# Issuing the mixer's pieces by an account of every tile's writes, reads and transfers

## The chip, the cores and the metric

The kernel runs on one core of a Trainium2 chip. It is one launch, and the time is the device time of that launch in microseconds (us). The core's engines run their own instruction streams in order and meet through semaphores: PE (the tensor engine, matmuls), DVE (the vector engine), ACT (the scalar engine), POOL (GpSimd) and SP, which here only issues DMA transfers. What is compared is the median of several runs of the kernel before and of the changed one.

## The reference

One block of an encoder on 16 meta tokens and 1024 frames of width 1024, in float32. The change lies in the token mixer, of which this is the core:

```python
def token_mixer(u, w_in, ..., w_out):
    proj = u @ w_in                       # q, k, v, o, gates of 4 mLSTM heads; q, k, v, g of 4 retention heads
    qk = silu(causal_dwconv(concat([ml_q, ml_k]), ml_conv_w))
    h_ml = mlstm_chunkwise(q, k, v, li, lf)            # li, lf: log gates, from 4 + 4 columns of proj
    h_ml = sigmoid(ml_o) * head_norm(h_ml, ml_norm_g)
    rq, rk = rotary(rt_q, pos), rotary(rt_k, pos)
    h_rt = retention_chunkwise(rq, rk, rv, log_gamma)
    h_rt = silu(rt_g) * head_norm(h_rt, rt_norm_g)
    return concat([h_ml, h_rt]) @ w_out
```

A gated feed-forward part (width 2816, with a causal convolution) and a last norm follow. They are not touched.

## The kernel before

**Products.** Every matrix product is done in float32 out of reduced-precision pieces: a matrix is split into a high part (an ACT cast, L365) and a low part (DVE, the matrix less its high part, L370), and a product takes three matmuls, high x high, low x high and high x low (L772, L773, L774). The large products use a seven-product scheme (Winograd's form of Strassen's): seven weights `hi_*`/`lo_*`, made from four quarters by sums (L443, L444, L447, L448 for one head's weights), meet seven right factors `uS1` to `uS4` and others. One **step** is one of those products over one range of tokens: 12 matmuls into one PSUM bank. `evac` (L838 to L844) then takes the bank away: a copy on ACT (L840, L842) for products 0, 6, 2, 3, a sum or difference on DVE (L844) for the rest.

**Stages.** After the input norm (to about 80 us) comes the mixer, head after head in the order 4, 0, 1, 2, 3, 5, 6, 7, where 0 to 3 are mLSTM heads and 4 to 7 retention heads. PE's steps run in a fixed order: `o` (the output gate of a head, banks `po4x`, `po4y`, ...), `q` (q and k of the next, `pq0x`, ...), `vp` (v of two heads, `pv1x`, ...), and so on; then the out-projection (`pwx`), up and gate, and down-projection, to the end.

**Pieces.** Between the steps goes all the rest, as **pieces**: the weight splits (`quartered`, L429ff, seven parts per weight); the convolution and Silu that make `qT` and `kT` (`qk_tasks`, L1001 to L1043); a retention head's rotary tables or an mLSTM head's decay tables (tiles `A`, loaded by `tables_load` L958, used by `tables_tasks`); the gate chain `gates()` (L1060ff, which on PE shows as the small tiles `pg`, `pe`, `pf` and `pt`); the chunkwise scan, `scan_a` (scores `s`, weighted scores `pt`) and `scan_b`; the head norm and, behind it, the transposes `tr` with the copies `mx` out of their one PSUM bank; sums of rows of `w_out` (`raw_w`, L515 to L519, stored back to DRAM as `wsw`); and two small groups on PE (`pvm` L596 and `pm`) that read a transferred weight unsplit.

**The order.** The program is written out by Python that runs once, and the order in which it emits the instructions is the order in which each engine runs them; no engine overtakes. `go` (L1567ff) takes the next PE step, and `slot` around it decides which pieces come ahead of and behind it. `tick` moves the weight pieces in `pend` and the pieces in `front` by one stage each; `side` holds the scan's pieces in a list, each with a condition. All of it goes by an **account**: `watch` sees every instruction and adds a time for it to a running sum for PE, DVE or ACT (`load`), so that `load["DVE"] - load["PE"]` tells how far DVE would be behind. It knows nothing of which tile an instruction reads. What is ready is stated by constants: a key in `done` holds from `max(load DVE, load ACT) + 0.3` on, a transfer is taken as landed after 4 us of PE work (`landed(4, ...)`) and a table after 9, the transpose bank as free 0.9 after the DVE sum, and the weights' own pieces wait only until their transfer was issued (`jwait`). Where a step needs a weight that isn't split yet, `need` (L385) sets `rush` and runs all the pieces there are, until that weight is there. `jload` issues the weight transfers on SP as soon as one of four buffers is free.

## Time and profile before

| | |
|---|---|
| runs, us | 1585.54, 1585.11, 1582.67; median 1585.11 |
| profiled execution, us | 1583.99, its span 1581.8, granted clock 0.98 of full |
| busy of the span | PE 95%, weight load 86%, DVE 69%, ACT 48%, POOL 5% |
| chain of work that ended last | PE 83%, DVE 7%, DMA 6%, ACT 3%, issue 1% |
| moved by DMA | 223.80 MB, mean 141 GB/s over the span |

In rows of the profile, `out<-in` are the tiles that an instruction writes and reads, with the numbers left out that tell apart the buffers of one name; L is the line in the program; `[4.09 <-DMA A<-rot_d]` behind a row is the idle time of its engine just before it, and what ended it. A row of the timeline begins with its start and its duration in us. SPq is SP's queue, in which rows are DMA issues, not transfers.

### The profile page before, as it was taken

Reading aid. Unit: us, or ns where it says so; the run is one execution under the profiler, and the core shown is the slowest. Engines: PE = TensorE matmul, PEld = TensorE weight load, DVE = VectorE, ACT = ScalarE, POOL = GpSimd, SP = SyncE. Lnnn points to the kernel's source line nnn. Section 1 sums busy time; section 2 is a strip of 40 time slices with the busy share of each in tenths; the row PEclk is TensorE's granted clock in tenths of the full one; section 3 lists DMA queues with packets and bytes.
Section 4 is the critical chain, followed back from the end, with each engine's and each line's share of the span. In section 5 each row is a group of like instructions: output and inputs, shape, how many; then the busy total and the mean of one; then the engine's idle time right before and its main releaser. Section 6 shows DMA issues by size and latency. Waiting matters only on the chain.

```text
span 1581.8 us, 25443 instructions
## 1 busy us (share of the span) xinstructions
PE 1505.7 (95%) x9929; PEld 1363.8 (86%) x9929; DVE 1093.4 (69%) x2107; ACT 756.6 (48%) x1454; POOL 72.3 (5%) x133
## 2 busy tenths in 40 slices
PE   7968998899899998998999999999999999999997
PEld 6958998899889998887787989999999999888887
DVE  7765686667775766583776878777666666678657
ACT  5445544545455454555344556444444444334443
POOL 1000000000000000000000000222220000000000
PEclk9979999999999999999999999999999999999998
DMA  6012245234632344469532416888883223943313
GB/s 224 1 59 77 77 138 187 81 97 126 200 112 78 110 150 153 133 231 374 187 120 77 147 51 207 211 219 205 196 190 99 80 81 97 386 142 100 95 52 107
DMA packets 104585, 223.80 MB, mean 141 GB/s; under 512 B 10520, under 2 KB 33760, under 8 KB 104288
## 3 DMA queue, kind: packets, MB, share of 16 engines
q1 hardware_dynamic: 95872, 199.02, 37.4%
q0 software_dynamic: 8448, 23.07, 7.3%
q8 instruction: 78, 1.28, 0.3%
q14 instruction: 43, 0.35, 0.1%
q10 hardware_dynamic: 144, 0.07, 0.0%
HBM read 178.05 MB, written 67.15 MB: 155 GB/s over the span
## 4 chain that ended last, share of the span: by engine, by line
PE 83%; DVE 7%; DMA 6%; ACT 3%; issue 1%; SPq 0%; DVEq 0%; ACTq 0%
PE pdx L774 3%; PE pdx L773 3%; PE pdx L772 3%; PE pup_x L773 2%; PE pup_x L774 2%; PE pup_x L772 2%; PE pga_x L772 2%; PE pga_x L773 2%; PE pga_x L774 2%; PE pdy L774 2%; PE pdy L773 2%; PE pdy L772 2%; PE pwx L774 2%; PE pv L812 2%; PE pwx L772 2%; PE pwx L773 2%
## 5 line engine op out<-in xcount | busy, mean ns | idle before, releaser
L656 ACT CAST hi_up<-raw_up 128x512 fp32r<-128x512 f32 (+1 forms) x52 | 36.5, 719 | 107.0 <-PE pga_z L773 60.2
L772 PE MATMUL pup_x<-uh_g,hi_up 128*128 128x256 f32 (+1 forms) x240 | 67.8, 285 | 1.2 <-ACT uh_g L1758 1.2
L773 PE MATMUL pup_x<-ul_g,hi_up 128*128 128x256 f32 (+1 forms) x240 | 67.9, 284 | 0.1
L657 DVE TENSOR_TENSOR lo_up<-raw_up,hi_up 128x512 fp32r<-128x512 f32 (+1 forms) x52 | 41.2, 808 | 38.4 <-ACT hi_up L656 37.7
L657 DVE TENSOR_TENSOR lo_ga<-fraw_ga,hi_ga 128x512 fp32r<-128x512 f32 (+1 forms) x52 | 41.8, 807 | 37.1 <-ACT hi_ga L656 36.9
L774 PE MATMUL pup_x<-uh_g,lo_up 128*128 128x256 f32 (+1 forms) x240 | 66.7, 284 | 0.0
L657 DVE TENSOR_TENSOR lo_d<-rd,hi_d 128x1024 fp32r<-128x1024 f32 (+1 forms) x34 | 37.6, 1112 | 32.8 <-ACT hi_d L656 32.7
L656 ACT CAST hi_ga<-fraw_ga 128x512 fp32r<-128x512 f32 (+1 forms) x52 | 36.4, 719 | 45.5 <-PE pup_z L773 24.1
L774 PE MATMUL pdx<-uh_d,lo_d 128*128 128x512 f32 (+1 forms) x156 | 57.9, 375 | 0.0
L773 PE MATMUL pdx<-ul_d,hi_d 128*128 128x512 f32 (+1 forms) x156 | 57.8, 374 | 0.0
L656 ACT CAST hi_d<-rd 128x1024 fp32r<-128x1024 f32 (+1 forms) x34 | 32.3, 959 | 49.4 <-PE pdy L773 32.5
L774 PE MATMUL pdy<-uh_d,lo_d 128*128 128x512 f32 x132 | 51.9, 393 | 0.0
L773 PE MATMUL pdy<-ul_d,hi_d 128*128 128x512 f32 x132 | 51.8, 392 | 0.0
L772 PE MATMUL pdx<-uh_d,hi_d 128*128 128x512 f32 (+1 forms) x156 | 48.5, 372 | 0.0
L772 PE MATMUL pdy<-uh_d,hi_d 128*128 128x512 f32 x132 | 47.9, 389 | 0.0
L772 PEld LDWEIGHTS pup_x<-uh_g,hi_up 128*128 128x128 f32 x240 | 45.9, 191 | 2.3 <-ACT uh_g L1758 1.4
L772 PE MATMUL pga_x<-uh_g,hi_ga 128*128 128x512 f32 x120 | 47.5, 396 | 0.0
L773 PE MATMUL pga_x<-ul_g,hi_ga 128*128 128x512 f32 x120 | 47.5, 396 | 0.0
L774 PE MATMUL pga_x<-uh_g,lo_ga 128*128 128x512 f32 x120 | 47.1, 393 | 0.0
L773 PEld LDWEIGHTS pup_x<-ul_g,hi_up 128*128 128x128 f32 x240 | 45.9, 191 | 1.0 <-DVE ul_g L1759 0.3
L774 PEld LDWEIGHTS pup_x<-uh_g,lo_up 128*128 128x128 f32 x240 | 45.1, 191 | 0.7
L1492 DVE SCALAR_TENSOR_TENSOR mx<-tr,vec,sig 128x386 f32<-128x386 f32 (+2 forms) x42 | 24.0, 571 | 31.2 <-PE tr L1484 21.0
(1684 smaller groups left out, 5788.0 us busy)
## 6 DMA issues: line engine op xcount, KB each, us to landing
raw_up<-w_up_d SPq DMA_DIRECT2D x22, 512.0 KB, 4.7
fraw_ga<-w_gate_d SPq DMA_DIRECT2D x22, 512.0 KB, 4.6
acts<-cv SPq DMA_DIRECT2D x44, 256.0 KB, 4.1
wsd<-w_down_d POOLq DMA_DIRECT2D x44, 256.0 KB, 6.5
rd<-wsd SPq DMA_DIRECT2D x22, 512.0 KB, 3.6
raw_w<-w_out_d SPq DMA_DIRECT2D x20, 512.0 KB, 4.3
wsw<-raw_w SPq DMA_DIRECT2D x32, 256.0 KB, 2.7
raw_m<-w_out_d SPq DMA_DIRECT2D x14, 512.0 KB, 4.6
```

Source lines behind the costliest of these rows:

```text
L656: AC.copy(hi[:, o:o + n], x)
L657: V.tensor_tensor(lo[:, o:o + n], x, hi[:, o:o + n].bitcast(F32), ALU.subtract)
L772: m.append(PE.matmul(pt, ah, xh_, start=first and k == 0, stop=False, skip_group_check=True))
L773: PE.matmul(pt, ah, xl_, start=False, stop=False, skip_group_check=True)
L774: m.append(PE.matmul(pt, al, xh_, start=False, stop=last and k == n - 1, skip_group_check=True))
L812: PE.matmul(pv[:, :nv], u[:, kb % 4, j0:j0 + L], (w0hi, w0lo)[j][kb // 4][:, o:o + nv], start=i + j + kb == 0, stop=i == 1 and kb == KB - ...
L1492: return V.scalar_tensor_tensor(dst, tr[:, x0 - t0:x1 - t0], vec[:, g:g + 1], sig(b, p)[:, x0 - a0:x1 - a0], ALU.mult, ALU.mult)
```

## The change

The computation, its tiles and its instructions stay what they are; what changes is the Python account, and by it the order. Of 9,464 instructions on PE 462 move, of 2,109 on DVE 298, of 1,457 on ACT 215, of 550 on SP 47, and on POOL none.

- A class `Slots` round every tile pool notes which buffer a tile lies in. `watch` keeps, for every buffer, the ranges that were written and read, by which engine and until when (`uses`), and lets an instruction start when its engine is free and all that it depends on has ended. SP, POOL and the transfers ("wire") get sums of their own; a transfer ends at the later of the wire and 1.8 us after its issue, plus its size over 0.3 MB per us (twice that for reads of `scr`).
- `fin` is the end of the latest instruction of a piece by that account. `done` holds `fin + 0.05`, and `landed` and the tables wait for the account's end of the transfer in place of 4 and 9 us. A weight's pieces now wait for that too.
- `tick` runs first the weight pieces that one of the next three weights belongs to, and passes over a piece until the PE's sum reaches the end of that piece's last stage.
- `need` no longer runs everything when a weight is late, only the pieces of weights up to that one; and `slot` issues scan pieces ahead of a PE step while the step's weight isn't ready.
- The three stages of `gates()` wait for what the stage before put on the engines (`settle`), and head 4's scan waits for the gates.
- `reset` clears the account at the mixer's start, with the ages of transfers.

```diff
-    load = {"PE": 0.0, "DVE": 0.0, "Activation": 0.0, "slot": 0.0}
-    RATE = {"PE": (0.004, 0.000445), "DVE": (0.12, 0.00098), "Activation": (0.1, 0.00083)}
+    load = {"PE": 0.0, "DVE": 0.0, "Activation": 0.0, "Pool": 0.0, "SP": 0.0, "wire": 0.0}
     before = {}
     TABLES = ("Sqrt", "Sigmoid", "Silu", "Exp")
     table = [None]
+    uses = {}
+    seen = [0]
+    fin = [0.0]
+    stalls = []
+
+    def extent(x):
+        y = getattr(x, "bass_ap", None)
+        if y is None:
+            return None
+        n = y.tensor.name
+        w = y.ap[0][0]
+        o = y.offset % w if n in tc.slots and w else 0
+        if n not in tc.slots:
+            return n, 0, 1
+        return tc.slots[n], o, o + 1 + sum(a * (k - 1) for a, k in y.ap[1:])
...
+        for e, w in [(e, False) for e in rd] + [(e, True) for e in wr]:
+            for lo, hi, wrote, at, by in uses.get(e[0], ()):
+                if lo < e[2] and hi > e[1] and (w or wrote):
+                    x = at if by == eng and not dma else at + 0.05
+                    if by == eng and not dma:
+                        continue
+                    if x > t:
+                        t, why = x, (by, e[0])
...
+        if dma:
+            load[eng] = t + 0.4
+            size = n * o.ap[0][1] * 4e-6
+            load["wire"] = max(load["wire"], t + 1.8) + size / 0.3 * (2 if "scr" in str(rd) else 1)
+            end = load["wire"]
...
+                if F32 not in [x.dtype for x in ins.ins]:
+                    c = max(0.107, 0.004 + 0.000445 * n)
+                elif o.ap[0][1] == 32:
+                    c = 0.13
+                elif getattr(ins, "is_transpose", False):
+                    c = 0.109
+                else:
+                    c = 2 * max(0.11, 0.00084 * n)
+                end = t + c + 0.165
+            elif eng == "DVE":
+                c = 0.07 + 0.00105 * n + (0.06 if "ScalarPtr" in kind else 0.0)
+                end = t + c + 0.085
+            elif eng == "Activation":
+                c = 0.045 + 0.00093 * n + 0.1 * (len(ins.ins) - 1)
+                f = ins.func.name if hasattr(ins, "func") else "Copy"
+                if f in TABLES and f != table[0]:
+                    table[0] = f
+                    c += 1.3
+                end = t + c + 0.1
+            else:
+                c = 0.15 + 0.0017 * n
+                end = t + c
+            load[eng] = t + c
+            fin[0] = max(fin[0], end)
...
-        age[i] = load["PE"]
...
+        age[i] = load["wire"]
...
-        while dealt[0] and not rush[0] and load["PE"] - max(age[i] for i in ids) < us:
+        while dealt[0] and not rush[0] and load["PE"] < max(age[i] for i in ids):
...
-    def spawn(g, q=pend):
+    until = {}
+    owner = {}
+    cursor = [0]
+
+    def spawn(g, q=pend, key=None):
         if dealt[0]:
             if next(g, pend) is not pend:
                 q.append(g)
+                until[id(g)] = fin[0]
+                owner[id(g)] = key
...
+        near = [g for g in pend if order.get(owner[id(g)], 10 ** 6) <= cursor[0] + 3]
+        for q in (near, front, pend):
             for g in list(q):
+                if q is pend and g in near:
+                    continue
                 if q is pend and not rush[0] and max(load["DVE"], load["Activation"]) - load["PE"] > 3:
                     break
+                if not rush[0] and until[id(g)] > load["PE"] + 0.5:
+                    continue
+                fin[0] = 0.0
                 if next(g, pend) is pend:
-                    q.remove(g)
+                    (pend if q is near else q).remove(g)
+                until[id(g)] = fin[0]
...
+    def settle():
+        t = fin[0]
+        yield
+        while dealt[0] and not rush[0] and load["PE"] < t:
...
-            self[key] = max(load["DVE"], load["Activation"]) + 0.3
+            self[key] = fin[0] + 0.05
...
-            rush[0] = True
             while key not in done:
-                tick()
-            rush[0] = False
+                n = seen[0]
+                rush[0] = True
+                for g in list(pend):
+                    if order.get(owner[id(g)], 10 ** 6) <= i0:
+                        fin[0] = 0.0
+                        if next(g, pend) is pend:
+                            pend.remove(g)
+                        else:
+                            until[id(g)] = fin[0]
+                rush[0] = False
+                if seen[0] == n and key not in done:
+                    rush[0] = True
+                    tick()
+                    rush[0] = False
...
-                yield from jwait(*(js[x] for x in {0: (0,), 1: (1,), 2: (0, 2, 3)}.get(i, (0, 1, 2, 3))))
+                yield from landed(*(js[x] for x in {0: (0,), 1: (1,), 2: (0, 2, 3)}.get(i, (0, 1, 2, 3))))
...
-                yield from landed(4, *js)
+                yield from landed(*js)
...
-            while not rush[0] and load["PE"] < tabs["at"] + 9:
+            while not rush[0] and load["PE"] < tabs["at"]:
...
-        yield
+        yield from settle()
...
-            return lambda: done.can(("qk", h, int(c > 4)), *([("tab", h)] if h < H else [])) and not (h == 7 and "meta" in done)
+            return lambda: done.can(("qk", h, int(c > 4)), *([("tab", h)] if h < H else ["gates"] if h == 4 else [])) and not (h == 7 and "meta" in done)
...
+        key = getattr(m, "key", None)
+        while key and not done.can(key) and able() and side[0][1] and load["DVE"] - load["PE"] < lim:
+            one()
```

The new `landed`, without the constant, stands likewise for the other pieces with transfers (`m_unit`, `w_unit`, `v_units` and the rows of the out-projection), and `done["tr"]` is `fin[0] + 0.05` in place of `load["DVE"] + 0.9`.

**SP at the start of the mixer.** `A_4_877` and `A_4_878` are the rotary tables of head 4, `raw_q0a` and `raw_q0b` the two halves of the q weights of head 0, `raw_vp_21` and `raw_vp_22` two quarters of the first v weights. Before:

```order
L241 DMA raw_q0a<-w_g_d 128x1024
L966 DMA A_4_877<-rot_d 128x1040
L967 DMA A_4_878<-rot_d 128x1040
L1129 DMA scr<-gates 36x128
L1131 DMA scr<-gates 36x128
L972 DMA A_0_1642<-scr 128x16
L973 DMA A_0_1642<-scr 128x8x128
L973 DMA A_0_1643<-scr 128x8x128
L241 DMA raw_vp_21_1310<-w_vp_d 128x1024
L241 DMA raw_vp_22_1312<-w_vp_d 128x1024
L241 DMA raw_q0b<-w_g_d 128x512 x2
```

Now:

```order
L296 DMA raw_q0a<-w_g_d 128x1024
L296 DMA raw_vp_21_1237<-w_vp_d 128x1024
L1053 DMA A_4_877<-rot_d 128x1040
L296 DMA raw_vp_22_1239<-w_vp_d 128x1024
L1054 DMA A_4_878<-rot_d 128x1040
L296 DMA raw_q0b<-w_g_d 128x512 x2
L1218 DMA scr<-gates 36x128
L1220 DMA scr<-gates 36x128
```

The two quarters of v now go ahead of the first and the second rotary table, and the second half of q0's weights right behind the tables, ahead of the two stores to `scr`.

**PE at the gate chain.** `pe` is the second small PE group of the gate chain; `po4x` and `po4y` are the banks of head 4's output gate. Before:

```order
L772 MATMUL po4x_881<-uS2h,hi_o_2_0_853 128x258
L773 MATMUL po4x_881<-uS2l,hi_o_2_0_853 128x258
L774 MATMUL po4x_881<-uS2h,lo_o_2_0_854 128x258
L1101 MATMUL pe<-cs,gates 1x36
L1102 MATMUL pe<-cs,gsm 1x36
L772 MATMUL po4x_895<-uS2h,hi_o_2_0_853 128x256
L773 MATMUL po4x_895<-uS2l,hi_o_2_0_853 128x256
L774 MATMUL po4x_895<-uS2h,lo_o_2_0_854 128x256
```

Now:

```order
L858 MATMUL po4y_913<-uS4h,hi_o_4_0_863 128x258
L859 MATMUL po4y_913<-uS4l,hi_o_4_0_863 128x258
L860 MATMUL po4y_913<-uS4h,lo_o_4_0_864 128x258
L1190 MATMUL pe<-cs,gates 1x36
L1191 MATMUL pe<-cs,gsm 1x36
L858 MATMUL po4y_930<-uS4h,hi_o_4_0_863 128x256
L859 MATMUL po4y_930<-uS4l,hi_o_4_0_863 128x256
L860 MATMUL po4y_930<-uS4h,lo_o_4_0_864 128x256
```

`pe` stood inside the third product of the output gate (`uS2`) and stands inside the sixth (`uS4`), 74 rows later.

**DVE in the middle of head 3.** `mx` are the copies of head 3's six transposes, `raw_w` the rows of `w_out` that are summed in place. Before:

```order
L1492 SCALAR_TENSOR_TENSOR mx_0_0_4645<-tr_0_0_4638,vec,sig 128x386
L370 TENSOR_TENSOR lo_q_5_0_4577<-raw_q3a,hi_q_5_0_4576 128x512
L1492 SCALAR_TENSOR_TENSOR mx_0_1_4670<-tr_0_1_4664,vec,sig 128x386
L515 TENSOR_TENSOR raw_w_4624<-raw_w_4624,raw_w_4622 128x512
L516 TENSOR_TENSOR raw_w_4622<-raw_w_4622 128x512
L1492 SCALAR_TENSOR_TENSOR mx_1_0_4695<-tr_1_0_4690,vec,sig 128x384
L518 TENSOR_TENSOR raw_w_4622<-raw_w_4622,raw_w_4624 128x512
L519 TENSOR_TENSOR raw_w_4624<-raw_w_4624,raw_w_4622 128x512
L370 TENSOR_TENSOR lo_o_0_0_4676<-raw_o3a,hi_o_0_0_4675 128x512
L1492 SCALAR_TENSOR_TENSOR mx_1_1_4718<-tr_1_1_4713,vec,sig 128x384
```

Now, from the third copy on, and then some twenty rows later:

```order
L1581 SCALAR_TENSOR_TENSOR mx_1_0_4701<-tr_1_0_4696,vec,sig 128x384
L930 TENSOR_TENSOR rawk<-rawk,pq3x_4521 128x248
L1581 SCALAR_TENSOR_TENSOR mx_1_1_4723<-tr_1_1_4718,vec,sig 128x384
L445 TENSOR_TENSOR lo_o_0_0_4654<-raw_o3a,hi_o_0_0_4653 128x512 x2
L930 TENSOR_TENSOR rawk<-rawk,pq3x_4549 128x264
L1581 SCALAR_TENSOR_TENSOR mx_2_0_4748<-tr_2_0_4744,vec,sig 128x256
...
L930 TENSOR_TENSOR sig<-sig,po3y_4882 128x256
L601 TENSOR_TENSOR raw_w_4728<-raw_w_4728,raw_w_4726 128x512
L602 TENSOR_TENSOR raw_w_4726<-raw_w_4726 128x512
L445 TENSOR_TENSOR lo_o_2_0_4753<-raw_o3a,hi_o_2_0_4752 128x512
```

The pair of sums (L515, L516 before; L601, L602 now), which read rows just transferred, stood between the second copy and the third and stands behind all of the six.

**ACT at the v weights of heads 2 and 3.** `hi_vp_2`, `hi_vp_3` and `hi_vp_4` are parts of these weights; the `ACTIVATE` rows take away the two banks of a product. Before:

```order
L840 COPY v_00_3598<-pv1x_3611 128x2x256
L365 CAST hi_vp_2_0_3653<-raw_vp_11_3357 128x512 x2
L365 CAST hi_vp_3_0_3727<-raw_vp_11_3357 128x512 x2
L842 ACTIVATE v_10_3757<-pv1x_3560 128x2x256
L842 ACTIVATE v_10_3757<-pv1x_3611 128x2x256
L365 CAST hi_vp_4_0_3789<-raw_vp_12_3364 128x512 x2
```

Now:

```order
L440 CAST hi_vp_2_0_3637<-raw_vp_11_3241 128x512 x2
L928 ACTIVATE v_10_3748<-pv1x_3524 128x2x256
L928 ACTIVATE v_10_3748<-pv1x_3580 128x2x256
L440 CAST hi_vp_3_0_3720<-raw_vp_11_3241 128x512 x2
L440 CAST hi_vp_4_0_3785<-raw_vp_12_3298 128x512 x2
L1102 ACTIVATE qT_3826<-rawq,vec 128x528
```

The casts of part 3 stood ahead of the two bank copies and stand behind them.

More of the change, by code (lines that the diff above doesn't have):

```diff
@@ L95, in watch @@
-        if nm not in RATE or not ins.outs or "DMA" in kind or "Tile" in kind:
+        eng, kind = ins.engine.name, type(ins).__name__
+        if "Tile" in kind or not ins.outs or eng not in load:
             return
-        if pinned[0] and nm in before:
-            tc.add_manual_dep(ins, before[nm], mybir.DependencyInfo(mybir.DependencyClass.NoSync, mybir.DependencyReason.DATA), reason="order")
-        before[nm] = ins.name
-        b, c = RATE[nm]
-        n = c * math.prod(x[1] for x in ins.outs[0].ap[1:])
@@ new lines, in watch @@
+        seen[0] += 1
+        if not dma and eng in ("PE", "DVE", "Activation"):
+            if pinned[0] and eng in before:
+                tc.add_manual_dep(ins, before[eng], mybir.DependencyInfo(mybir.DependencyClass.NoSync, mybir.DependencyReason.DATA), reason="order")
+            before[eng] = ins.name
+        o = ins.outs[0]
+        n = math.prod(x[1] for x in o.ap[1:])
+        rd = [e for e in map(extent, ins.ins) if e]
+        wr = [e for e in map(extent, ins.outs) if e]
+        t = load[eng]
@@ L484, in tail_sum @@
             V.tensor_tensor(tail, tail, pt[:, :2 * P], ALU.add)
-        done["tr"] = load["DVE"] + 0.9
+        done["tr"] = fin[0] + 0.05
         done.discard("meta")
@@ L598, in g @@
                 yield from quads(vz[:META, s * 264:s * 264 + DV], pv, DV)
-                done["tr"] = load["DVE"] + 0.9
+                done["tr"] = fin[0] + 0.05
                 done.discard("meta")
```

93 lines of the change are left out of this document (57 added, 36 removed).

## The prediction

> **What bounds the kernel now.** I read the totals first, then the busy time of each engine in stretches of the program, then what the PE (TensorE) waited for in the stretch that the change touches, then those waits in order of time.
>
> ```profile
> PE 1505.7 (95%) x9929; PEld 1363.8 (86%) x9929; DVE 1093.4 (69%) x2107; ACT 756.6 (48%) x1454; POOL 72.3 (5%) x133
> 80.00:150.00 70.00, 50.53 (x347) 46.59 (x346) 37.73 (x103) 31.00 (x63) 0.21 (x2) 0.83 0.24 77
> 150.00:300.00 150.00, 139.07 (x1092) 130.09 (x1090) 107.47 (x238) 77.45 (x162) 2.81 (x15) 0.99 0.38 123
> 300.00:450.00 150.00, 142.91 (x1125) 136.38 (x1125) 106.02 (x245) 81.79 (x172) 3.44 (x18) 1.00 0.39 124
> 450.00:600.00 150.00, 148.67 (x1165) 140.36 (x1164) 101.79 (x238) 73.39 (x156) 1.64 (x9) 0.99 0.38 124
> 600.00:760.00 160.00, 145.91 (x1003) 131.31 (x1003) 99.70 (x221) 81.02 (x166) 0.00 (x0) 0.96 0.60 210
> ```
>
> Columns of the stretches: from:to, length, then busy microseconds of PE, weight load, DVE, ACT, POOL, the granted clock, the DMA share and GB/s. The PE is the bound. Every matmul of before is still there, so a changed order can only win idle PE time and half-clock time of the mixer, which runs from about 80 to 760: 19.5 + 10.9 + 7.1 + 1.3 + 14.1 = 53 us idle, plus what the clock loses.
>
> ```profile
> PE pe L1101 <- DVE gates L1094: 14.6, 1, 14.6
> PE tr L1484 <- DVE mx L1492: 11.2, 8, 4.7
> PE s L1376 <- ACT kT L1029: 5.9, 2, 3.0
> PE s L1376 <- DVE pt L1400: 5.7, 3, 4.2
> 88.50:98.80 10.30, 0.01 (x1) 0.04 (x1) 7.46 (x25) 6.88 (x10) 0.00 (x0) 0.50 0.00 0
> 98.80:109.00 10.20, 9.55 (x45) 8.70 (x46) 4.52 (x22) 3.64 (x9) 0.21 (x2) 0.50 0.02 4
> 259.20:262.60 3.40, 3.40 (x17) 3.40 (x17) 2.23 (x4) 1.67 (x4) 0.10 (x1) 0.50 1.03 387
> ```
>
> The waits give total, times and longest. The clock column shows what an idle spell costs behind itself: after the longest, the PE works another 10.2 us at half clock and loses half of the 9.55 busy, 4.8 us; after the 4.7 us wait that ends at 259, one stretch of 3.4 us, 1.7. The same 0.50 stands in one such stretch each after the waits at 128, 449, 614, 621 and 650. I use 1.7 us for a spell.
>
> **The change part by part. (1) The gates.** PE waits 14.6 us for the gate chain on DVE, and DVE for the rotary tables:
>
> ```profile
> 80.72 0.33 SPq L241 DMA_DIRECT2D raw_q0a<-w_g_d  x1
> 82.57 0.33 SPq L966 DMA_DIRECT2D A<-rot_d  x1
> 82.60 0.28 PE L772 MATMUL po4x<-uS2h,hi_o 128*128 128x258 f32 x1
> 82.72 0.28 PE L773 MATMUL po4x<-uS2l,hi_o 128*128 128x258 f32 x1
> 87.80 0.71 DVE L1042 TENSOR_TENSOR qT<-rawq,A 128x528 f32<-128x528 f32 x1 [4.09 <-DMA A<-rot_d]
> 89.06 0.71 DVE L1043 TENSOR_TENSOR kT<-kT,A 128x528 f32<-128x528 f32 x1 [0.55 <-DMA A<-rot_d]
> 93.17 0.41 DVE L844 TENSOR_TENSOR sig<-sig,po4y 128x258 f32<-128x258 f32 x1
> 99.66 0.22 PE L1102 MATMUL pe<-cs,gsm 36*1 36x36 f32 x1 [0.65 <-DVE gsm L1098]
> 114.37 1.07 PE L596 MATMUL pvm<-raw_vm,ug 128*32 128x256 f32 x16
> DMA packets 432, 1.59 MB, mean 132 GB/s; under 512 B 48, under 2 KB 48, under 8 KB 432
> ```
>
> The change puts seven Winograd steps of 12 matmuls (0.12 us from start to start, 1.44 a step) and the small pvm group between pg and pe instead of two steps. That does not free the PE. Its fourth step from pg, po4y with uS1, second chunk, overwrites a bank that DVE L844 must have read, and that L844 stands behind the same tables. The PE gets there at 82.6 (where uS2 starts now) + 1.1 (pvm) + 3 x 1.44 = 88; the L844 ends at 93.6 if the tables land as now. Two weight transfers of 512 KB now stand in SP's order ahead of the first and second table. Here 1.59 MB moved from 80.7 to 89.1, 0.19 MB/us, so these 1.05 MB more in front cost up to 5.5 us; the last row of the clock fence (387 GB/s) moves twice that, 2.8 us; and nothing is lost if it is hidden in the 5.2 us to landing. I take 3: L844 ends at 96.6, PE idle 8.6 (5.6 to 11.1). Then DVE has some 15 us of queued work while the PE has ten steps at a clock partly halved: 1.3 more, and 3.4 for the clock (1.7 to 4.8). Left 13.3 of 14.6 + 0.65 + 4.8 = 20.0: **-6.7** (-11 to -3).
>
> The Trainium skill, "DMA: Bandwidth & Descriptors", section Queues, rings and completion order, says that each DMA engine takes the descriptors of a queue in ring order. That speaks against this part of the change: by it alone both tables land behind both weight parts, and this term would be -4.2, with 5.5 in place of 3. The rows of before cannot show it, since nothing of size stood ahead of the tables.
>
> **(2) The late half of q0's weights** held DVE, and with it the PE's next score:
>
> ```profile
> 126.83 0.69 DVE L443 TENSOR_TENSOR raw_q0b<-raw_q0b 128x512 f32<-128x512 f32 x1 [7.58 <-DMA raw_q0b<-w_g_d]
> ```
>
> Now raw_q0b is issued right behind the tables, some 40 us before 126.8, and its first reader comes some 70 DVE rows after the gates began. The 4.2 us above and a spell: **-5.9** (-5.9 to 0).
>
> **(3) raw_w blocks DVE** in two heads, with the copy out of the transpose bank queued behind it, and the next transpose behind that:
>
> ```profile
> 242.80 7.91 DMA wsw<-raw_w
> 250.72 6.15 DMA raw_w<-w_out_d
> 257.06 0.69 DVE L515 TENSOR_TENSOR raw_w<-raw_w,raw_w 128x512 f32<-128x512 f32 x1 [4.81 <-DMA raw_w<-w_out_d]
> 428.12 0.55 PE L1484 MATMUL tr<-cs,v 128*128 128x128 f32 x3 [3.34 <-DVE mx L1492]
> ```
>
> In head 3 the pair L515/L516 moves behind all six copies. In head 0 it stays behind the first of them, but its distance from the previous sums grows to nine PE steps and their pieces, 16 us, against the 14 us that the store and the load take (first two rows). 4.7 + 3.34 + 1.7: **-9.7** (-9.7 to -4).
>
> **(4) The first score of heads 1 and 3** waits for the Silu of kT. It moves six steps of 1.44 us back, more than the 5.9 us that both waited together; with one half-clock spell **-7.6** (-7.6 to -3). Given back: the weights of o1's step S1 become late.
>
> ```profile
> 265.29 2.36 DVE L1018 SCALAR_TENSOR_TENSOR qT<-rawq,vec,qT 128x527 f32<-128x527 f32 x3
> 275.42 0.69 DVE L370 TENSOR_TENSOR lo_o<-raw_o1a,hi_o 128x512 fp32r<-128x512 f32 x1
> ```
>
> From the last copies of head 0 on, DVE has two such convolutions, the mask of the tables, eight rows like the second and some 2 us of copies ahead of their end, 13 us, and starts 0.9 after the PE; the PE has 10.7 us, a transpose and seven steps. 13 + 0.9 - 10.7 is about 3, and a spell: **+4.7** (0 to 6).
>
> **(5) The late weights of o6 and q7:**
>
> ```profile
> PE pq7x L774 <- DVE lo_q L370: 2.1, 1, 2.1
> PE po6x L774 <- DVE lo_o L370: 1.9, 1, 1.9
> PE pq7y L774 <- DVE lo_q L370: 1.3, 1, 1.3
> PE po6y L772 <- ACT hi_o L365: 1.0, 1, 1.0
> ```
>
> 6.3 us, and three half-clock spells: 11.4 us. The weights move only a few rows: in q7 the sums go ahead of four scan rows, in o6 one unit of the right factor goes behind. I take three quarters of it: **-8.5** (-11.4 to 0).
>
> **(6) A new wait at v1, step S1.** The two ACT casts of its weights move behind the second copy of the previous product, which waits for the PE's last matmul of that step:
>
> ```profile
> 349.32 1.14 ACT L365 CAST hi_vp<-raw_vp 128x512 fp32r<-128x512 f32 x2 [5.04 <-DVE raw_vp L448]
> 351.88 0.60 ACT L842 ACTIVATE v<-pv1x 128x512 f32<-128x512 f32 x1 [0.92 <-PE pv1x L774]
> 349.97 1.29 DVE L370 TENSOR_TENSOR lo_vp<-raw_vp,hi_vp 128x512 fp32r<-128x512 f32 x2 [0.69 <-ACT hi_vp L365]
> 351.68 0.27 PE L772 MATMUL pv1y<-hi_vp,uS1h 128*128 128x256 f32 x1
> ```
>
> Today the step starts just when its lo part is done. Behind the copy (351.88 + 0.60) come 1.14 and the rest of 1.29 us: some 3.4 late, and a spell: **+5.1** (2 to 8).
>
> **(7) Crowding.** Head 4's transposes now come in adjacent pairs, each waiting for the copy between: +1.5; at the end of the mixer two pairs lose cover: +1 (0 to 6 together).
>
> The sum: -6.7 - 5.9 - 9.7 - 7.6 + 4.7 - 8.5 + 5.1 + 2.5 = -26.1. Some 300 other PE and 300 other DVE rows move, and each place where the new order is denser can hold a wait that no row of before shows. The nearest measure is a quiet stretch and a busy one of the same work, 450 to 600 with 1.3 us idle and 300 to 450 with 7.1: I add 4.1 (0 to 12). **Forecast -22 us**, on the profiled execution's 1583.99 us (its span and 2.2 around it), 1562; the median of the runs lies 1.1 above that execution, so **1563**.
>
> The Trainium skill, "TensorE: Matmul & The Clock Gate", Part 1, gives one busy window of about 3.4 us as enough to return to full clock. The 3.4 us spells agree; the 10.2 us of 98.8 to 109 do not. By the page 1.7 us of clock would be gone with the gates' wait instead of 4.8, 3.1 less.
>
> **The rivals.** *The waits only move.* The head's pieces start later everywhere, and the DVE work behind them (69% busy) meets the next weights. For: two weight parts, o1 and v1, get later, by rows above. Against: DVE idles 43 us of each 150. Then (4) and (5) bring nothing and the unseen waits reach 10 us: -26.1 + 7.6 + 8.5 + 10 = 0, and -7 with half of that loss; 1578 to 1585, as one number 1580. *Transfers arrive later than the account has them.* The old code waited a fixed 4 or 9 us of PE work before a piece with a transfer; the new one lets it go at 1.8 us plus size over 0.3 MB/us, 3.5 us for 512 KB. The rows say up to twice that:
>
> ```profile
> wsw<-raw_w SPq DMA_DIRECT2D x8, 256.0 KB, 7.6
> A<-scr SPq DMA_DIRECT2D x2, 512.0 KB, 8.5
> ```
>
> Then PE's pvm and pm groups and DVE's raw_w and table rows block in their engines' order: 6 + 7 + 8 + 4 such units. At 1.5 us of PE each that is +37, and 1584 - 22 + 37 = 1599; it decides the sign once a unit costs more than 0.9 us. Against: raw_w was late twice in before too, with the fixed wait. *More is won.* The tables hide behind the peak rate, (5) is won whole, (4)'s and (6)'s new waits vanish in slack: -11 - 5.9 - 9.7 - 7.6 - 11.4 + 2.5 = -43, 1542; half of that gain on top of the forecast is 1552.
>
> **How the numbers follow.** Forecast 0.60, its own range 1553 to 1573 (terms 3 to 7 between their near bounds). The waits only move 0.16. Late transfers 0.12, nearly all of it slower. More is won 0.12. About 0.2%, 3 us, is what the measurement can tell from no change: that takes in a third of the moving-waits case, 0.05. Slower 0.12, faster 0.83. The range 1546 to 1584 leaves out most of the late-transfer case and the best half of the last.
>
> **What would show each step.** (1) PE idle of 6 to 11 us before a po4y matmul with uS1, released by DVE L844's successor, no long wait at pe; right if A<-rot lands after 89. (2) No DVE wait on raw_q0b. (3) No raw_w wait ahead of mx. (4) No wait of s on kT's Silu; one before po1y. (5) Waits before po6x, po6y, pq7 under 4 us in all. (6) About 3.5 us before pv1y. Wrong would be: PE or DVE rows released by DMA raw_w, raw_m, raw_vm or A<-scr adding to more than 10 us, or a mixer whose idle sum between the same matmuls is not below 40 us.

## The result, and the profile after

The changed kernel takes 1573.18 us, the median of four runs (1569.85 to 1576.01), against 1585.32 before: a ratio of 0.9924, 95% interval 0.9897 to 0.995. That is 12 us where 22 were forecast, inside the range. The profiled execution of the changed kernel took 1569.85 us, span 1567.6. Two executions of those below are left out of the medians and ratios: one of e12 (1640.46 us, granted clock 0.86) and one of the kernel before, run beside e13 (3764.03 us).

First, the two stretches of each kernel that begin with the mixer's first output-gate matmul and with the first matmul of the out-projection (from:to, length, busy time of PE, weight load, DVE, ACT and POOL, granted clock, DMA share, GB/s). Before:

```profile
75.85:733.12 657.27, 605.53 (x4641) 569.22 (x4639) 441.20 (x1010) 333.40 (x696) 8.86 (x45) 0.97 0.40 134
733.12:1581.80 848.68, 834.82 (x4819) 731.38 (x4819) 596.19 (x996) 388.30 (x703) 55.64 (x79) 0.99 0.50 150
```

After:

```profile
78.16:721.85 643.69, 604.72 (x4646) 568.58 (x4645) 441.01 (x1013) 334.44 (x697) 9.88 (x45) 0.98 0.42 135
721.85:1567.60 845.75, 831.49 (x4813) 728.98 (x4813) 595.42 (x993) 388.34 (x702) 55.61 (x79) 0.99 0.50 151
```

The mixer is 13.6 us shorter: its idle time, length less busy time of the PE, fell from 51.7 to 39.0 us. The rest is 2.9 us shorter, of which 2.3 us lie between the first pwx and the first pwy matmul of the out-projection. The start, which the change does not touch, came 2.3 us later in this execution; in the executions below it lies between 74.4 and 78.2.

What the PE waited for between 75 and 760 us (total, times, longest), to be held against the rows of before in the prediction:

```profile
PE po4y L858 <- DVE sig L930: 8.4, 1, 8.4
PE s L1465 <- DVE pt L1489: 6.4, 2, 4.1
PE u L1513 <- DVE vz L1507: 6.2, 4, 3.0
PE tr L1573 <- DVE mx L1581: 4.8, 6, 1.8
PE po1y L860 <- DVE lo_o L445: 2.9, 1, 2.9
PE po1x L860 <- DVE lo_o L445: 1.8, 1, 1.8
...
PE pq0x L858 <- DVE sig L930: 1.5, 1, 1.5
PE pwx L858 <- ACT hi_w L742: 1.5, 1, 1.5
PE pv1y L858 <- ACT hi_vp L440: 1.2, 1, 1.2
PE pv1y L859 <- DVE lo_vp L445: 1.1, 2, 0.8
PE po3y L860 <- DVE lo_o L445: 1.1, 1, 1.1
```

Gone are the waits at pe, of s on kT, and before the weights of o6 and q7. The 8.4 us before po4y and the late weights of o1 were forecast. Two rows were not: `u` on `vz`, which before does not have, and `s` on `pt`, longer than before by 0.7 us in total and no longer at the same places: 2.35 us in head 5 and 4.06 in head 6, where before had 0.51 and 0.94 (and, in head 4, the 4.23 of term 2, which is gone).

### The profile page after: what moved, and what is told of

It is laid out like the page before. It is cut to its first block, busy times and chain, and to the rows that moved or that the text cites. A ratio compares the mean times of both kernels' runs of the same rounds, so it can differ in the third digit from the quotient of the medians.

```text
span 1567.6 us, 25461 instructions
## 1 busy us (share of the span) xinstructions
PE 1503.6 (96%) x9929; PEld 1362.7 (87%) x9929; DVE 1092.4 (70%) x2107; ACT 757.7 (48%) x1454; POOL 73.3 (5%) x133
## 4 chain that ended last, share of the span: by engine, by line
PE 87%; DVE 7%; DMA 3%; ACT 2%; issue 1%; SPq 0%; DVEq 0%; ACTq 0%
PE pdx L860 3%; PE pdx L859 3%; PE pdx L858 3%; PE pup_x L859 2%; PE pup_x L860 2%; PE pga_x L858 2%; PE pup_x L858 2%; PE pga_x L859 2%; PE pga_x L860 2%; PE n L1515 2%; PE pdy L860 2%; PE pdy L859 2%; PE pdy L858 2%; PE u L1513 2%; PE pv L898 2%; PE pwx L860 2%
## 5 line engine op out<-in xcount | busy, mean ns | idle before, releaser
L743 DVE TENSOR_TENSOR lo_up<-raw_up,hi_up 128x512 fp32r<-128x512 f32 (+1 forms) x52 | 41.3, 810 | 38.2 <-ACT hi_up L742 37.4
L859 PE MATMUL pdy<-ul_d,hi_d 128*128 128x512 f32 x132 | 51.7, 392 | 0.0
```

The source lines that it names most:

```text
L743: V.tensor_tensor(lo[:, o:o + n], x, hi[:, o:o + n].bitcast(F32), ALU.subtract)
L859: PE.matmul(pt, ah, xl_, start=False, stop=False, skip_group_check=True)
```

## The experiments

Three numbers are read from each profile for the mixer as bounded above: its length, the PE's idle time in it, and the clock loss, the sum over slices of 1.7 us of busy time x (1 - granted clock). What is left, the work at full clock, is 591 to 594 us in every kernel but one (596), so idle time and clock loss explain the lengths. Each ratio is to runs of the kernel before taken beside that kernel; their medians lie between 1583.2 and 1585.3.

| kernel | median us | ratio to before, 95% | mixer us | idle | clock loss |
|---|---|---|---|---|---|
| before | 1585.3 | 1 | 657.3 | 51.7 | 14.6 |
| the change | 1573.2 | 0.9924 (0.9897 to 0.995) | 643.7 | 39.0 | 12.3 |
| the change again (after_again) | 1571.3 | 0.9926 (0.99 to 0.9952) | 642.7 | 38.2 | 12.4 |
| before, with the gate part (e10) | 1570.3 | 0.9918 (0.9896 to 0.9941) | 644.0 | 40.2 | 13.3 |
| without the gate part (e13) | 1576.2 | 0.9947 (0.9928 to 0.9966) | 651.0 | 45.8 | 11.9 |
| old order within a tick (e7) | 1596.0 | 1.0074 (1.0051 to 1.0096) | 671.0 | 54.6 | 20.3 |
| old transfer constants (e5) | 1577.1 | 0.9967 (0.9947 to 0.9987) | 654.5 | 44.9 | 16.0 |
| old forced path (e6) | 1571.7 | 0.9924 (0.99 to 0.9949) | 639.0 | 39.4 | 6.8 |
| ones on GpSimd (e1) | 1561.5 | 0.9856 (0.9827 to 0.9885) | 636.5 | 34.8 | 8.5 |
| tables first (e3) | 1565.7 | 0.9889 (0.9854 to 0.9923) | 639.3 | 37.1 | 9.8 |
| rotary products late (e11) | 1568.7 | 0.9893 (0.9866 to 0.9919) | 643.9 | 33.1 | 19.3 |
| second score waits (e12) | 1571.3 | 0.9919 (0.9898 to 0.9939) | 644.5 | 39.8 | 12.2 |
| ones and tables (c1) | 1558.4 | 0.9842 (0.9816 to 0.9869) | 632.5 | 30.6 | 9.0 |
| c1 with a margin (c2) | 1567.3 | 0.9897 (0.9879 to 0.9915) | 643.9 | 36.3 | 14.9 |

The profiled execution is one of the runs and need not be their median.

### The measure

> The changed kernel unchanged, as the measure for the others of this chip: 1573, between 1568 and 1577. In a second profile the idle time of the PE in the mixer is the same within 2 us at the same places, while the half-clock stretches behind the waits of about 1 us may differ by one or two of 1.7 us.

It came out so: 1571.27, idle 38.2 against 39.0. Its nine runs lie between 1565.55 and 1583.13, so a difference of 3 us between two kernels is not told from none by the time alone; there the waits decide.

### The gate part alone, in the kernel before

```diff
-        yield
+        yield from lag(8)
         pe = ps.tile([P, 512], F32, tag="sA", bufs=1, name="pe")
...
-            return lambda: done.can(("qk", h, int(c > 4)), *([("tab", h)] if h < H else [])) ...
+            return lambda: done.can(("qk", h, int(c > 4)), *([("tab", h)] if h < H else ["gates"] if h == 4 else [])) ...
```

(the other two stages likewise, with 2 and 4 us)

> The kernel before, with one part of the change alone: the three stages of the gate chain come 8, 2 and 4 us of PE work later, and head 4's scan waits for the gates. 76 rows of PE move, around the gates; raw_q0b is then issued ahead of the gates' stores and its first reader comes after pe. Theory A (terms 1 and 2 of the prediction stand by themselves): the 14.6 us wait at pe becomes one of 6 to 9 us before po4y, the 4.2 us wait behind raw_q0b goes with its half-clock stretch, and all later waits stay as in the kernel before (tr on mx 4.7 and 3.3, s on kT 5.9, o6 and q7 7): the mixer is 12 to 15 us shorter, 1569 to 1572. Rival B (the pieces that are put off meet the next weights, and the gain is given back by the end of head 0): the mixer is at most 6 us shorter, 1578 to 1584.

Theory A. The waits of the PE in its profile:

```profile
PE tr L1484 <- DVE mx L1492: 9.7, 9, 2.9
PE po4y L772 <- DVE sig L844: 7.8, 1, 7.8
PE s L1376 <- ACT kT L1029: 5.6, 2, 3.0
PE pwx L772 <- ACT hi_w L656: 3.3, 1, 3.3
PE pq7x L774 <- DVE lo_q L370: 2.1, 1, 2.1
PE po6x L774 <- DVE lo_o L370: 2.0, 1, 2.0
PE pf L1120 <- ACT gsm L1117: 1.5, 1, 1.5
```

The 14.6 us at pe became 7.8 before po4y, and the wait behind raw_q0b is gone; kT, o6 and q7 wait as in the kernel before; the two waits behind raw_w, 4.75 and 3.34 us there, are 2.45 and 2.90. The mixer is 13.3 us shorter. The whole change makes it 13.6 shorter. So this one part, 76 moved rows of the PE and the earlier raw_q0b with them, is worth as much as the change: all its other parts together come out at nothing.

### The change without its gate part

```diff
-                if not rush[0] and until[id(g)] > load["PE"] + 0.5:
+                if not rush[0] and g not in soon and until[id(g)] > load["PE"] + 0.5:
...
-        yield from settle()
+        yield
...
+    soon.append(gate_gen)
```

> The changed kernel with its gate part alone undone: the stages of the gate chain are issued at once, as in the kernel before, so that pe stands again inside the third product of the output gate; SP's order stays that of the change, with raw_q0b early. Theory A (the gate part is worth what the prediction gave it, about 7 us, in any company, and the other parts keep the rest of the gain): a wait of 14 to 17 us at pe is back, the one of 8.3 us before po4y is gone, no wait behind raw_q0b: 1577 to 1581. Rival B (without the gate part nothing of the gain is left, because the rest of the change gives back what it wins): 1582 to 1587, the kernel before. Rival C (the pieces find room under the long wait): 1570 to 1575.

Between A and C, nearest to A: 14.42 us at pe, none before po4y, none behind raw_q0b, and a mixer 7.3 and 8.3 us longer than the change's two. 1576.17 is 1 us under A's range. Two of its waits:

```profile
PE pe L1191 <- DVE gates L1184: 14.4, 1, 14.4
...
PE pq5x L859 <- ACT vz L871: 3.0, 1, 3.0
```

The gate term of the prediction, 6.7, fits both kernels as a whole. At the place itself it fits e10 (15.2 us idle became 7.8 + 1.5, and the clock loss 4.8 became 3.7: 7.1 in all). Here the idle time at the gates is 5.2 us longer than in the change and the clock loss about 1.0 smaller, some 4 in all; the rest lies at waits that this order puts elsewhere, the longest the one before pq5x, with others gone. What is left against before, 6.3 us of mixer, is about the 5.9 of raw_q0b, which this kernel keeps: again nothing remains for the other parts.

### The order within a tick

```diff
-        near = [g for g in pend if order.get(owner[id(g)], 10 ** 6) <= cursor[0] + 3]
-        for q in (near, front, pend):
+        for q in (front, pend):
...
-                if not rush[0] and until[id(g)] > load["PE"] + 0.5:
-                    continue
```

> The changed kernel with the old rule for the pieces between steps: the scan's pieces first, then all weight pieces in turn, none passed over until the PE's sum reaches its last stage; the account stays. Theory A (weight parts of the next three weights going first is what took the waits at q0, o6 and q7 away): waits on hi_ and lo_ weights come back at four places and more, 8 us of idle and as many half-clock stretches, 1583 to 1593. Rival B (the account's times alone do it, the order within a tick matters little): 1569 to 1577.

Theory A, past its upper end: 1596.02, slower than before. The waits of the PE in its profile:

```profile
PE po4y L853 <- DVE sig L925: 9.9, 1, 9.9
PE tr L1568 <- DVE mx L1576: 7.3, 10, 2.0
PE pq2x L855 <- DVE lo_o L440: 4.3, 1, 4.3
PE pq5x L855 <- DVE lo_o L440: 4.3, 1, 4.3
PE po6x L853 <- ACT hi_o L435: 3.5, 1, 3.5
PE pq7x L855 <- DVE lo_q L440: 3.3, 1, 3.3
```

Late weights stop the PE at q2, q5, o6 and q7. So the waits at o6 and q7 went because of the new rule within a tick; with the rest of the change alone they are longer than before (3.5 and 3.3 us, where before had 1.9 and 2.1). The edit takes away two things at once, that the next weights' parts go first and that a piece is passed over until its last stage has ended; which of them did it isn't shown.

### The transfer constants

```diff
-        age[i] = load["wire"]
+        age[i] = load["PE"]
...
-        while dealt[0] and not rush[0] and load["PE"] < max(age[i] for i in ids):
+        while dealt[0] and not rush[0] and load["PE"] - max(age[i] for i in ids) < us:
...
-                yield from landed(*(js[x] for ...
+                yield from jwait(*(js[x] for ...
...
-            while not rush[0] and load["PE"] < tabs["at"]:
+            while not rush[0] and load["PE"] < tabs["at"] + 9:
```

> The changed kernel with the old constants for transfers in place of the account's end of the transfer: 4 us of PE work for rows that are read unsplit, 9 for the tables, and none for the weights. Theory A (the account's transfer times are what took the waits on raw_w and raw_q0b away): DVE waits on raw_w of 3 us and more come back in at least two heads, with the PE's wait for tr <- mx behind them, and weights late by their transfer: +8 to +15, 1581 to 1588. Rival B (order of the pieces alone did it, the transfer times matter little): DVE's waits on transfers stay below 2 us in all behind the rotary tables, 1570 to 1577.

Neither. The mixer is 10.8 us longer than with the change, as A has it, while the median is only 3.9 above the change's (6.8 by the two ratios). But not one wait on raw_w came back. One row of DVE's timeline (start, duration, and in brackets the idle time ahead of it) holds most of it:

```profile
284.40 0.69 DVE L529 TENSOR_TENSOR raw_q2b<-raw_q2b 128x512 f32<-128x512 f32 x1 [6.42 <-DMA raw_q2b<-w_g_d]
```

DVE takes up a weight part 6.4 us before its transfer lands, and u, whose `vz` stands behind it, waits 7.49 us. The new wait for a weight's transfer does something; the waits on raw_w went through the order of the pieces, as the prediction's third part argued, and not through the account's transfer times. This kernel also issues the tables ahead of the weight parts again, and its wait before po4y is 6.1 us in place of 8.4.

### The forced path

In `need`, the loop of the change is replaced by the three lines of before (`rush` on, `tick`, `rush` off).

> The changed kernel with the old forced path: where a weight is not ready, all pieces are run at once, not only those of weights up to that one. Theory A (the forced path acts only where it is taken, around o1 and v1, and the gain at o6 and q7 comes from the order of the weight pieces): o6 and q7 stay without a wait, o1 or v1 get 1 to 4 us worse, 1573 to 1577. Rival B (the forced path is what made o6 and q7 late before): waits before po6x, po6y, pq7x, pq7y come back to 4 us and more, 1580 to 1585.

Theory A: no wait before o6 or q7; the wait before v1 is 2.2 in place of 1.2 us, those before o1 are 2.3 + 1.8, 0.7 us less than the change's 1.8 + 2.9. In time no difference is seen. The profiled execution was a quick one, 1561.53, with the same waits: its clock loss is 6.8 us in place of 12.3.

### The first u of a head

Where the new wait comes from is seen in the changed kernel's DVE and PE timelines:

```profile
195.00 0.69 DVE L601 TENSOR_TENSOR raw_w<-raw_w,raw_w 128x512 f32<-128x512 f32 x1 [0.39 <-DMA raw_w<-w_out_d]
...
196.94 0.28 DVE L1484 TENSOR_TENSOR pt<-s,A 128x128 f32<-128x128 f32 x1
197.14 0.28 DVE L1487 TENSOR_TENSOR qd<-qT,A 128x128 f32<-128x128 f32 x1
197.34 0.69 DVE L604 TENSOR_TENSOR raw_w<-raw_w,raw_w 128x512 f32<-128x512 f32 x1
198.06 0.69 DVE L605 TENSOR_TENSOR raw_w<-raw_w,raw_w 128x512 f32<-128x512 f32 x1
198.67 0.69 DVE L533 TENSOR_TENSOR raw_o0a<-raw_o0a 128x512 f32<-128x512 f32 x1
199.39 0.69 DVE L534 TENSOR_TENSOR raw_o0a<-raw_o0a,raw_o0b 128x512 f32<-128x512 f32 x1
...
200.04 0.06 DVE L1507 MEMSET vz<- 16x1 f32 x1
200.17 1.22 PE L1513 MATMUL u<-vz,kw 16*128 16x257 f32 x2 [2.98 <-DVE vz L1507]
```

`scan_b` issues a memset of a column of ones and, right behind it, the matmul u that reads it. The memset takes 0.06 us and needs nothing, but it stands at the end of DVE's queue, behind four sums that now go first, and the PE waits for all of them.

```diff
-                    V.memset(vz[:META, VZ[h] * 264 + DV:VZ[h] * 264 + VW], 1.0)
+                    G.memset(vz[:META, VZ[h] * 264 + DV:VZ[h] * 264 + VW], 1.0)
```

(`watch` goes on counting it as DVE's, so that the order stays)

> The changed kernel with one thing else: the 16x1 memset of ones in vz, which the first state product u of each mLSTM head reads and which stands at the end of DVE's queue, is done by GpSimd; every other instruction keeps its place on its engine. Theory A (the new order's own waits give back part of the gain, and each can be taken away by itself): the four waits of u on vz, 2.98 + 1.54 + 0.92 + 0.80 = 6.2 us in the changed kernel's profile, go, and with them two half-clock stretches of 1.7 us: 1573 - 9 = 1564, profile about 1561. Rival B (the waits only move, because DVE behind them is full): the PE stops at the next thing that DVE owes it, at most 3 us are won, 1570 to 1573, and the idle sum of the mixer stays at 38 to 41 us.

Theory A: 1561.52. All four waits are gone, and the half-clock stretches behind the first and third are gone too. Little took their place; two short waits are new:

```profile
PE po0y L862 <- DVE sig L934: 0.7, 1, 0.7
PE po6x L864 <- DVE lo_o L449: 0.6, 1, 0.6
```

With these, and 0.8 us more before o1 and q0, the idle time fell by 4.2 us where the four waits were 6.2. The mixer of the profiled execution is 7.2 and 6.2 us shorter than the change's two, and the median lies 9.8 and 11.7 us under the change's two medians. So a memset of 0.06 us was worth 6 to 12 us.

### The tables ahead of the weight parts

```diff
+            if rotated and nm in ("vp0_21", "vp0_22"):
+                after(m, rotated[0])
...
-            nc.sync.dma_start(A2, rot[:, 1])
+            x = nc.sync.dma_start(A2, rot[:, 1])
+            if h == 4:
+                rotated.append(x)
```

> The changed kernel with the two weight parts vp0_21 and vp0_22 held behind the two rotary tables in SP's order, as in the kernel before; PE, DVE and ACT keep their order in the mixer. Theory A (the PE's 8.4 us wait before po4y is the tables' landing, and the weight parts ahead of them on the queue cost part of it, 3 us by the prediction): the second table lands as long after its issue as before, 5.3 us in place of 7.3, the wait is 2 to 3 us shorter, 1570 to 1571. Rival B (the order of the issues does not matter, the same bytes share the engines): the wait stays at 8.0 to 8.8 us, 1573.

Theory A for the wait: 6.1 us before po4y in place of 8.4. The DVE rows that wait for the second table, here and in the change:

```profile
88.58 0.71 DVE L1138 TENSOR_TENSOR kT<-kT,A 128x528 f32<-128x528 f32 x1 [1.21 <-DMA A<-rot_d]
```

```profile
94.38 0.71 DVE L1132 TENSOR_TENSOR kT<-kT,A 128x528 f32<-128x528 f32 x1 [2.12 <-DMA A<-rot_d]
```

From its issue that is 5.8 us (82.76) here and 7.3 us (87.06) in the change. The first table took 5.1 us here and 5.4 in the change, with a 512 KB part issued ahead of it. The median is 1565.66, 4 us below what A gave, but the five runs spread over 14 us; c1 tells more.

### Both together, and a margin

> The changed kernel with both single edits that won time: the memset of ones on GpSimd and the two weight parts held behind the rotary tables in SP's order; PE, DVE and ACT keep their order in the mixer. Theory A (two losses at separate places add up): the mixer's idle time is 38.5 - 6 - 2.2 = 30 to 31 us, 1559, between 1556 and 1562. Rival B (they overlap): 1561 to 1565.

Theory A: 1558.37, idle 30.6. The two losses lie at separate places and add up. This kernel is faster than both, 0.9842 of the time before.

In the next one `Ready.add` has `fin[0] + 0.3` in place of 0.05.

> The kernel with the two edits and, besides, pieces taken as ready 0.3 us after the account's end in place of 0.05; 152 rows of PE move. Theory A (the account is right but a little early, and a margin spares short waits): the idle sum is 1 to 4 us lower than without the margin, 1555 to 1558. Rival B (the margin only shuffles the order): within 3 us of the kernel without it, either way.

Neither: it is 8.9 us slower than without the margin. The margin takes away the waits before po1x and po1y (2.2 + 3.0 us) and puts others in their place: 1.80 us before pq1x and 3.01 + 0.93 + 0.71 + 0.80 of tr on mx, with a longer clock loss. A rule's constant moves 150 rows, and what that brings isn't to be had from the constant.

### The second score of heads 5 and 6

```diff
-... ["gates"] if h == 4 else [])) and not (h == 7 and "meta" in done)
+... ["gates"] if h == 4 else []), *([("pre", h, c - 1)] if h in (5, 6) and c == 1 else [])) and not ...
```

> The changed kernel with one condition more: the second score of heads 5 and 6 is issued only when the account has the first one's bank read by DVE (pt done). 141 rows of PE move, from head 5 on. Theory A (the waits of s on pt, 2.35 and 3.95 us in the changed kernel's second profile, are own losses like those of u on vz): both go, and the half-clock stretch of 1.7 us behind the second: 1572 - 8 = 1564. Rival B (here DVE is full with the weight parts, so the PE then waits for weights): waits on lo_ weights of o5, q6 or o6 of 4 to 6 us come in their place, 1570 to 1574.

Rival B: 1571.27. The waits of s on pt are gone and others have come, in the same profile:

```profile
PE po6y L860 <- DVE lo_o L445: 2.1, 1, 2.1
...
PE po6x L860 <- DVE lo_o L445: 1.3, 1, 1.3
...
PE pq7x L860 <- DVE lo_q L445: 1.1, 1, 1.1
```

together with 1.74 us of tr on mx: 6.2 us for 6.3 to 6.4. What the longer of the two waits was is seen in the changed kernel:

```profile
612.07 0.69 DVE L534 TENSOR_TENSOR raw_o6a<-raw_o6a,raw_o6b 128x512 f32<-128x512 f32 x1
612.68 0.23 DVE L1489 SCALAR_TENSOR_TENSOR pt<-s,cs 128x16 f32<-128x16 f32 x1
612.96 0.80 PE L1465 MATMUL s<-qT,kT 128*128 128x128 f32 x2 [4.06 <-DVE pt L1489]
```

`pt` stands behind the sums of o6's own weights, and DVE is busy for 12.6 of the 13 us from 600 on, in both kernels. So at o6 the change had itself moved a wait: 3.7 us before po6x and po6y became these 4.06 of s on pt, and this edit moves part of it back. Unlike the memset, the wait only moved. An order that puts `pt` ahead of those sums was not tried.

### The rotary products behind the gate chain

```diff
+            yield from lag(14 if (h, i, r) == (4, 0, 0) else 0)
             yield
...
-    side += qk_tasks(4)[:2] + gate_tasks + qk_tasks(4)[2:] + scan[:12]
+    side += gate_tasks + qk_tasks(4) + scan[:12]
```

> The changed kernel, with head 4's first rotary products, the DVE rows that wait for the tables, put 14 us of PE work later, behind the gate chain; 14 rows of PE and 30 of DVE move, and the account is told when the tables land, which its reset had forgotten. Theory A (what is left of the gate term is DVE waiting for the tables with the bank sum sig <- sig, po4y behind them): the 8.4 us wait before po4y falls below 2 us, and its half-clock stretch of 2.7 us goes; 9 to 11 us faster than the changed kernel, 1562 to 1564. Rival B (the DVE work is only put off): q0's weights or head 4's scores come late instead, by 4 us and more, and at most 5 us are won, 1568 to 1573.

In this kernel head 4's later rotary products read q and k after head 0's first product has begun to replace them; its instructions and their durations are those of the change. A for the cause, between A and B for the time: the 8.3 us before po4y are gone, so it was the tables that the bank sums stood behind (`reset` had cleared their transfers from the account, and the change issued these products as if the tables were there); a wait of 3.17 us of s on pt in head 4 came, and the idle time fell by 5 us. The clock loss of this execution, 19.3 us, hides that gain: half-clock stretches of 10.2 us stand behind the new wait and of 6.8 behind three shorter ones. It is no way to a faster kernel, since the products have to be done before head 0's.

## Point by point

The sizes are from the two profiles; clock losses from slices of 0.85 us at the place.

| step | forecast | measured, before to after |
|---|---|---|
| (1) gates | -6.7 | idle 15.2 to 8.4 + 1.5 (pq0x), clock 4.8 to 2.7: -7.5 |
| (2) raw_q0b | -5.9 | 4.2 + 1.7 to 0: -5.9 |
| (3) raw_w | -9.7 | 4.75 + 3.34 + 1.6 to 1.8: -7.9 |
| (4) kT; o1's weights | -7.6; +4.7 | -7.6; 1.8 + 2.9 + 1.1 (po3y) + 1.6 clock: +7.4 |
| (5) o6 and q7 | -8.5 | 7.0 + 4.8 to 0: -11.8 |
| (6) v1 | +5.1 | 1.2 + 1.1 + 1.7 clock: +4.0 |
| (7) crowding | +2.5 | other tr on mx 3.1 to 3.0, pv0x 0 to 1.0: +0.9 |
| waits that no row shows | +4.1 | u on vz 6.2 + 4.9 clock, s on pt 5.0 + 1.6 clock: +17.7 |
| not forecast | 0 | pwx 3.3 to 1.5, pm 1.3 to 0.3, v of head 7 0.7 to 0, waits under 0.3 us 0.8 to 0.2: -4.2 |

The sum of the right-hand column is -14.9. By the table above, the mixer's idle time fell by 12.8 and its clock loss by 2.3, 15.1 together, and its work at full clock came out 1.5 longer. The clock parts belong to these two executions: in the change's second profile they are 6.8 for u and none for v1.

The **sign and the mechanisms** were right. The wait moved from pe to po4y at the length that was worked out (8.6 forecast, 8.4 measured), through the tables and the bank sum behind them; o1's and v1's weights became late; raw_q0b, raw_w, kT, o6 and q7 stopped being waited for. Single sizes are off by 0 to 3.3 us: without the unseen waits the forecast was -26.1, and the same seven terms measure -28.4.

**The step that failed** is the last one of the sum, "each place where the new order is denser can hold a wait that no row of before shows", sized at 4.1 from the idle time of a quiet and a busy stretch, with 12 as its end. It was 17.7. Comparing stretches of before was the wrong measure, since both stretches were made by the old rule, under which the memset stood right behind `qd` in all four heads (from 198.27 to 198.51 in head 0). The rows were there to be found: in the new order of DVE four sums stand between `qd` and the memset that u reads, 4 x 0.69 us, and that is nearly all of the 2.98 us. e1 shows that this loss was the change's own, and avoidable; in e12 the other one, s on pt, moves to other places with a full DVE.

**The rival "the waits only move"** was given 0.16 at 1580, and describes terms (3) to (7): with e10 and e13 the gate part and raw_q0b hold the whole gain, 13.3 of 13.6 us, and the 27 us won at raw_w, kT, o6 and q7 were given back by new waits. It fell short in that (5) was won whole at its own rows, though at o6 s on pt took its place (e12). By the prediction's own test, an idle sum not below 40, the case is at the edge: 39.0. **Late transfers** did not happen: behind the tables, DVE waited 0.4 us on raw_w and on no other weight. **More is won** did not happen: with two more edits, c1 is at 1558.

**SP's order.** Counted from raw_q0a's issue the second table landed 8.3 us later before, 11.3 in the change and 9.1 in e3: 3.0 us for the two weight parts, as taken, of which 2.2 hang on the order. The prediction says that nothing of size stood ahead of the tables before, and puts both parts ahead of both tables; but raw_q0a, 512 KB, was ahead of them in both kernels, and only one part was ahead of the first table. The Trainium skill, "DMA: Bandwidth & Descriptors", section Queues, rings and completion order, says that descriptors of one queue are taken in ring order, which the prediction priced at 5.5. The trace agrees in part: the second table, with two parts ahead, landed 1.5 to 2 us later from its issue than without them, in e3 and in the kernel before; the first, with one part ahead, 0.2 to 0.3.

## What to carry to other kernels

When an order changes, take each matmul that writes or reads a tile touched by a queue-tail instruction, however small, and count what stands ahead of that instruction on its engine: a 0.06 us memset behind four sums held the PE for 2.98 us, and its like for 6.2 us over four heads. Before crediting a rewrite with its gain, do its parts alone: here one delay of three stages held nearly all of it. In this kernel a wait on an instruction that an idle engine could do was taken away; one on a full engine only moved.

## What was not expected of the hardware

**The clock does not answer a short wait in the same way each time.** The waits of 1.19 us before pv1y in two executions of the changed kernel, with the stretch behind each (granted clock is the third number from the end):

```profile
347.90:353.60 5.70, 5.25 (x29) 5.06 (x30) 5.55 (x9) 2.82 (x6) 0.00 (x0) 0.70 0.48 157
349.30:353.60 4.30, 4.30 (x26) 4.30 (x25) 4.23 (x7) 1.42 (x3) 0.00 (x0) 0.60 0.63 207
```

```profile
346.30:350.60 4.30, 3.95 (x31) 3.75 (x32) 4.30 (x7) 2.63 (x5) 0.00 (x0) 1.00 0.42 127
```

In the first, a half-clock stretch begins some 2 us after the wait ended, in the second none. Over the mixers of all profiles such stretches last about 3.4, 6.8 or 10.2 us (two, which take in the 14 us waits at pe, 13.7 and 20.5). The change lost 12.3 and 12.4 us of clock in its two executions, in part at different places, and e6 with nearly the same waits 6.8. Most of the spread between runs of one kernel goes with the clock: in the nine of after_again its mean falls from 0.987 in the quickest (1565.55) to 0.974 in the slowest (1583.13), and 0.013 of the PE's 1504 busy us is, as an estimate, 20 us. Waits of 4 us and more brought such a stretch each time, in all profiles.

**The return to full clock does not go by the length of the wait.** After the 8.4 us before po4y the PE worked at half clock from 98.95 to about 104.3, 5.4 us (first row), where before it was 10.2 us after 14.6. But e13, after 14.4 us at pe, was back after 4.0; and behind the s on pt of head 6 it took 3.4 us in the change (4.06 us of wait) and 11.0 in c1 (3.73), up to 607.7, with the PE busy throughout (second row, of c1). The Trainium skill, "TensorE: Matmul & The Clock Gate", Part 1, has one busy window of about 3.4 us for it; the 3.4 us agree, the 10.2 and 11.0 do not.

```profile
98.95:104.50 5.55, 5.55 (x26) 5.55 (x27) 5.33 (x13) 5.43 (x11) 0.00 (x0) 0.51 0.17 53
604.79:606.49 1.70, 1.70 (x10) 1.70 (x9) 1.06 (x4) 1.35 (x4) 0.00 (x0) 0.50 0.06 24
```
